# The MLP's steady part of a two-stream hybrid layer: a scheduler's order, and an order written out by hand

## The chip, the cores and the metric

The kernel runs on one core of a Trainium2 chip. The metric is the time of one execution on the device in microseconds (us). The core has a matmul engine (TensorE, PE in the profile, with its weight loads shown apart as PEld), VectorE (DVE), ScalarE (ACT), GpSimd (POOL) and SyncE (SP), which here only starts DMAs. GpSimd starts the DMAs that add to what lies in the buffer. Each engine works through its own queue in order.

## The reference, cut to what matters

One layer is computed for two streams at once, 128 context rows and 512 latent rows, 640 columns in the kernel's transposed layout, with 1024 channels in float32. Three mixers run on an input projection; their outputs are merged, projected by w_out and added to the stream. Then comes the gated MLP, which the change is about (D_FF is 2816, dw_conv is a centred depthwise convolution of width 3):

```python
x = x + gt1 * (merged @ w_o)
h2 = rms_norm(x, n2) * (1 + sc2) + sh2
u_val, u_gate = jnp.split(dw_conv(h2 @ w_up, f_conv), 2, axis=-1)
x = x + gt2 * ((jax.nn.silu(u_gate) * u_val) @ w_dn)
```

## The kernel before

Each float32 matrix product is made of three products of rounded halves: every operand is split into a high part and the rest, and high*high, rest*high and high*rest are accumulated in PSUM. For a weight tile, w_split (L149, L150) casts on ScalarE (wh from raw) and subtracts on VectorE (wl). Weight tiles are loaded by w_load (L140) and st_load (L248 to L252).

The 2816 MLP columns are 22 tiles of 128, f = 0 to 21, in blocks of 4, 4, 4, 4, 3 and 3. The first block (up_tile) is done plainly. From f = 4 on, up_pair makes a value tile and its gate tile together, from seven half-size products of 12 matmuls instead of eight, on sums of weights and sums of activations; the bodies below call them, in order, X, Y, Z, X, Y, Z, Y. Four weight tiles (st, j = 0 to 3) feed a pair; the second and the third hold two sums of weights, of which one is made in flight: SyncE loads a piece (L248), and GpSimd's DMA adds another onto it (L250). VectorE makes the other sums (st_sums: L258 for j = 0, which needs tile 0 and the accumulated half of tile 1, and L260 for j = 2). Three raw buffers and two pairs of wh and wl turn over.

The products are evacuated by ScalarE (L1708, L1718: the copies of X) and VectorE (L1711 to L1733) into two tiles u1 (value) and u2 (gate). finish then convolves each (conv: L506 on ScalarE and four steps, L508, on VectorE), applies the gate (gated: L1651, L1652) and splits the result (split_x: L398, L399).

Between pairs, down multiplies the block before with a 128-row tile of w_down: 24 matmuls for a block of four, 18 for a block of three (gemm_p, L365), and adds the result to the residual stream x1 (two instructions on VectorE, L1759, xa in the rows). A pair is followed by two downs, in the last two blocks by two, three and three; the weights are rawd, whd and wld, two buffers each. At the end, eight downs follow for the last block, each with five transposes (L613), two copies (L1767) and two output DMAs.

What sets the order of the work: all five queues are filled by a scheduler, which goes by dependences and priorities. W looks ahead in a plan of weights (loads up to LOOK_F = 6 ahead where may_load finds a buffer, splits one ahead) and gives loads and splits high priority, as up_pair gives the evacuations. The convolutions and the gate of a pair are a generator, of which some() issues a piece at four places of the next pair.

Of the kernel before, what the change touches and what calls it, by code (L numbers as in the profile page):

```python
# [12 lines left out]
AF = mybir.ActivationFunctionType  # L13
# [45 lines left out]
def hybrid_step(ctx: ExitStack, tc: tile.TileContext, a: dict, o: list):  # L59
# [170 lines left out]

    pidx = {g[0]: i for i, g in enumerate(plan)}
    loaded, split = {}, {}
    LOOK_L, LOOK_S, LOOK_F = 2, 1, 6
    used = [0]


# [3 lines left out]
    def st_load(f, j):  # L240
# [11 lines left out]
            SY.dma_start(out=hi, in_=part(0, 1))  # L252
        return raw

    def st_sums(f, j):

        if j == 0:
            V.tensor_add(st_raw[f, 0][:, 512:], st_raw[f, 0][:, :512], st_raw[f, 1][:, :512])  # L258
        elif j == 2:
            V.tensor_add(st_raw[f, 2][:, 512:], st_raw[f, 0][:, 512:], st_raw[f, 1][:, 512:])  # L260

    def load_of(j):
        key, pieces, kt, n = plan[j]
        return st_load(*key[1:]) if key[0] == "st" else w_load(pieces, kt, n, key[0] == "wd")
# [4 lines left out]
            st_sums(*key[1:])  # L269
        return w_split(loaded[j], kt, n, key[0] == "wd")  # L270

    def may_load(j):

        down = plan[j][0][0] == "wd"
        same = [i for i in range(j) if (plan[i][0][0] == "wd") == down]
        n = 2 if down else RAWB
        if len(same) < n:
            return down
        i = same[-n]
        if i not in split:  # L280
            return False
        key = plan[i][0]
        return key[0] != "st" or key[2] > 1 or pidx["st", key[1], 2] in split

    def W(key):
        i = pidx[key]
        assert i == used[0], (key, i, used[0])
        used[0] += 1
        with tc.high_priority() if i else nullcontext():
            for j in range(i, min(i + LOOK_L + 1, len(plan))):  # L290
                if j not in loaded:
                    loaded[j] = load_of(j)
            for j in range(i, min(i + LOOK_S + 1, len(plan))):
                if j not in split:
                    split[j] = split_of(j)
            if key[0] in ("uv", "ug", "st", "wd"):
                for j in range(i + LOOK_L + 1, min(i + LOOK_F + 1, len(plan))):
                    if j not in loaded:
                        if not may_load(j):
                            break  # L300
                        loaded[j] = load_of(j)
        return split[i]


# [1244 lines left out]
    def ft():  # L1549
        return fslots.pop(0)  # L1550
# [137 lines left out]
            hs[k, i] = rt(2)  # L1688
            split_x(t, *(u[:, :T] for u in hs[k, i]))

    def up_pair(f):

        ps = gtile()
        X, Y, Z = ps[:, :HALF], ps[:, 512:512 + HALF], stile()[:, :HALF]
# [7 lines left out]

        hH2 = h2H, h2L
        u1, u2 = ft(), ft()
        w = W(("st", f, 0))
        prod(X, w, 0, lambda j, k: hH2[j][:, k, L], True, False)
        with tc.high_priority():
            S.copy(u2[:, L], X)  # L1708
        prod(Y, w, 1, lambda j, k: hs[k, 1][j][:, R], True, False)
        with tc.high_priority():  # L1710
            V.tensor_sub(u1[:, R], u2[:, L], Y)  # L1711
        w = W(("st", f, 1))
        prod(Z, w, 0, lambda j, k: hs[k, 0][j][:, L], True, False)
        with tc.high_priority():
            V.tensor_add(u2[:, R], u2[:, L], Z)
        prod(X, w, 1, lambda j, k: hH2[j][:, 4 + k, L], False, True)
        with tc.high_priority():
            S.copy(u1[:, L], X)  # L1718
        some()
        w = W(("st", f, 2))  # L1720
        prod(Y, w, 0, lambda j, k: hs[k, 0][j][:, R], False, False)
        with tc.high_priority():
            V.tensor_sub(u2[:, R], Y, u2[:, R])
        some()
        prod(Z, w, 1, lambda j, k: hH2[j][:, 4 + k, R], False, True)
        with tc.high_priority():
            V.tensor_add(u1[:, R], u1[:, R], Z)
        some()
        some()
        w = W(("st", f, 3))  # L1730
        prod(Y, w, 0, lambda j, k: hs[k, 1][j][:, L], False, True)
        with tc.high_priority():
# [48 lines left out]
    e1x.close()  # L1781
    e2 = ctx.enter_context(tc.tile_pool(name="e2", bufs=1, reuse_waits="tile"))
    slots.extend(e2.tile([P, T + 2], F32R, name=f"r{i}") for i in range(24, 32))
    for b in range(1, NB_F):
        for i in range(FBLK[b]):
            up_pair(fst[b] + i)
            for nt in downs(b, i):
                down(b - 1, nt)
    while later:
        some()  # L1790
    for nt in range(8):
        down(NB_F - 1, nt)


# [32 lines left out]
```

## Time and profile before

| | |
|---|---|
| median of three runs | 1421.82 us (1420.29 to 1423.12) |
| profiled execution | 1424.66 us |
| its span | 1422.9 us |
| TensorE busy | 1330.2 us, 93% |
| VectorE busy | 891.1 us, 63% |
| ScalarE busy | 578.9 us, 41% |
| GpSimd busy | 217.7 us, 15% |
| DMA | 137.97 MB, 97 GB/s in the mean |

The profile is that of one execution; its span is counted from the first to the last thing on the core, and the execution's own time is 1.8 us longer. A matmul's end is modelled, and neighbours overlap, so the spacing of starts tells more than durations. The part that the change is about begins at about 983 us with the first pair and goes to the end of the span.

### The profile page before, as it was taken

To read this page: it belongs to the slowest core of one execution; us is meant where nothing else is said; L and a number is where in the kernel's file an instruction comes from. 1 tells how busy PE (TensorE), PEld (TensorE's weight loads), DVE (VectorE), ACT (ScalarE), POOL (GpSimd) and SP (SyncE) were. 2 spreads that over 40 slices of the span, in tenths; PEclk is the share of its full clock that TensorE was granted. 3 is DMA by queue.
4 is the path that set the end of the run, shared out by engine and by line. 5 is a ranking of instruction groups with operands and counts; after the bars stand their busy time and mean duration, and the time that the engine had idled before them with its cause. 6 is when DMAs were issued, how large, how long until landed. Compare 5 with 4: busy or idle time off the path is not lost.

```text
span 1422.9 us, 27064 instructions
## 1 busy us (share of the span) xinstructions
PE 1330.2 (93%) x10985; PEld 1243.6 (87%) x10985; DVE 891.1 (63%) x1863; ACT 578.9 (41%) x1080; POOL 217.7 (15%) x224
## 2 busy tenths in 40 slices
PE   5999899998989899999999999989899999999898
PEld 4899899998878788999998898988898888988887
DVE  4675876785788553344343344498768677676764
ACT  4543334422675432343333234474334333333333
POOL 1011112203215211012120041100110111101000
PEclk9999999999999999999999999999999999999999
DMA  9523331222011144344344535222544545544323
GB/s 283 151 60 94 82 79 42 56 81 62 20 43 38 39 106 126 91 110 123 85 136 141 149 96 161 70 67 41 114 112 104 104 119 106 109 112 95 94 65 110
DMA packets 228079, 137.97 MB, mean 97 GB/s; under 512 B 22037, under 2 KB 221491, under 8 KB 227955
## 3 DMA queue, kind: packets, MB, share of 16 engines
q1 hardware_dynamic: 208563, 126.48, 32.7%
q0 software_dynamic: 19008, 9.44, 5.4%
q8 instruction: 86, 1.41, 0.4%
q10 hardware_dynamic: 384, 0.33, 0.1%
q14 instruction: 38, 0.31, 0.1%
HBM read 129.67 MB, written 6.55 MB: 96 GB/s over the span
## 4 chain that ended last, share of the span: by engine, by line
PE 50%; DVE 17%; DMA 10%; issue 5%; ACT 3%; POOL 3%; ACTq 0%; SPq 0%; POOLq 0%; DVEq 0%
PE g L365 30%; DMA raw<-in_w_up_dram 9%; PE g L1700 5%; DVE t L508 4%; DVE wl L150 3%; PE g L386 2%; PE s L1700 2%; DVE xa L1759 1%; PE s L613 1%; PE s L413 1%; PE s L1439 1%; DVE wld L150 1%; PE s L1427 1%; ACT wh L149 1%; POOL ssn L335 1%
## 5 line engine op out<-in xcount | busy, mean ns | idle before, releaser
L149 ACT CAST wh<-raw 128x1024 fp32r<-128x1024 f32 (+1 forms) x176 | 164.7, 945 | 358.4 <-PE g L365 179.4
L150 DVE TENSOR_TENSOR wl<-raw,wh 128x1024 fp32r<-128x1024 f32 (+1 forms) x176 | 192.3, 1101 | 153.3 <-ACT wh L149 143.3
L365 PE MATMUL g<-hH,wh 128*128 128x320 f32 x768 | 186.8, 322 | 3.4 <-ACT wh L149 1.9
L365 PE MATMUL g<-hL,wh 128*128 128x320 f32 x768 | 183.9, 317 | 0.0
L365 PE MATMUL g<-hH,wl 128*128 128x320 f32 x768 | 182.3, 316 | 0.0
L365 PE MATMUL g<-r,whd 128*128 128x320 f32 x704 | 139.2, 317 | 10.8 <-DVE t L1733 8.7
L365 PEld LDWEIGHTS g<-hH,wh 128*128 128x128 f32 x768 | 129.1, 191 | 11.5 <-issue 3.9
L365 PEld LDWEIGHTS g<-hL,wh 128*128 128x128 f32 x768 | 130.7, 191 | 2.5 <-issue 1.9
L365 PEld LDWEIGHTS g<-hH,wl 128*128 128x128 f32 x768 | 131.1, 191 | 2.0 <-issue 1.8
L365 PEld LDWEIGHTS g<-r,whd 128*128 128x128 f32 x704 | 111.8, 191 | 16.7 <-DVE t L1733 12.9
L250 POOL DMA_DIRECT2D raw<-in_w_up_dram x36 | 46.4, 1290 | 386.9 <-DMA raw<-in_w_up_dram 294.2
L1700 PE MATMUL g<-r,wh 128*128 128x320 f32 x432 | 101.6, 321 | 3.7 <-ACT t L1708 3.7
L386 PE MATMUL g<-wh,hH 128*128 128x256 f32 x320 | 95.0, 297 | 3.4 <-DVE xb L721 3.4
L386 PE MATMUL g<-wl,hH 128*128 128x256 f32 x320 | 94.5, 295 | 0.0
L386 PE MATMUL g<-wh,hL 128*128 128x256 f32 x320 | 94.5, 295 | 0.0
L1700 PEld LDWEIGHTS g<-r,wh 128*128 128x128 f32 x432 | 70.4, 188 | 12.8 <-ACT t L1708 7.6
L365 PE MATMUL g<-r,wld 128*128 128x320 f32 x352 | 81.0, 311 | 0.0
L508 DVE SCALAR_TENSOR_TENSOR t<-t,fcols,t 128x511 f32<-128x511 f32 (+1 forms) x156 | 78.5, 543 | 3.4 <-ACT t L506 2.9
L365 PE MATMUL g<-oz,wh 128*128 128x320 f32 x384 | 73.8, 314 | 1.3 <-DVE xb L1300 1.2
L386 PEld LDWEIGHTS g<-wh,hH 128*128 128x128 f32 x320 | 63.3, 198 | 5.2 <-DVE xb L721 3.6
L1700 PE MATMUL g<-r,wl 128*128 128x320 f32 x216 | 66.7, 309 | 0.0
L386 PEld LDWEIGHTS g<-wl,hH 128*128 128x128 f32 x320 | 63.7, 199 | 0.0
(592 smaller groups left out, 2902.3 us busy)
## 6 DMA issues: line engine op xcount, KB each, us to landing
raw<-in_w_in_dram SPq DMA_DIRECT2D x64, 512.0 KB
raw<-in_w_up_dram SPq DMA_DIRECT2D x90, 256.0 KB
wada<-in_w_ada_dram SPq DMA_DIRECT2D x32, 512.0 KB
raw<-in_w_up_dram POOLq DMA_DIRECT2D x36, 256.0 KB, 4.7
wat<-in_w_ada_dram SPq DMA_DIRECT2D x16, 512.0 KB
rawd<-in_w_down_dram SPq DMA_DIRECT2D x32, 256.0 KB
raw<-in_w_branch_dram SPq DMA_DIRECT2D x24, 256.0 KB
raw<-in_w_out_dram SPq DMA_DIRECT2D x8, 512.0 KB
```

What stands on the lines that cost most here:

```text
L149: S.copy(wh[:, :m], raw[:, :m])
L150: V.tensor_sub(wl[:, :m], raw[:, :m], wh[:, :m].bitcast(F32))
L250: G.dma_start(out=lo, in_=part(1, 2 - j), accum_op=ALU.add)
L335: G.tensor_tensor(out=out, in0=out, in1=mh.broadcast_to([P, n]), op=ALU.pow)
L365: PE.matmul(out=ps[:, OFF + c0:OFF + c1], lhsT=ww[:, k, :], rhs=xx(k)[:, c0:c1], start=(k == 0 and i == 0), stop=(k == kt - 1 and i == 2))
L386: PE.matmul(out=ps[b][:, o:o + GRP], lhsT=xx[:, 4 * kh + k, cs], rhs=ww[:, k, :], start=(kh == 0 and c % 2 == 0 and k == 0 and i == 0), st ...
L413: PE.matmul(out=pa[32 * g:32 * g + 32, :w], lhsT=csil[:, k, :], rhs=t[g], start=start, stop=stop)
L508: V.scalar_tensor_tensor(out=y[:, o0:o1], in0=src[:, i0:i0 + o1 - o0], scalar=w3(t), in1=y[:, o0:o1], op0=ALU.mult, op1=ALU.add)
L613: PE.transpose(pt[:, i * P:(i + 1) * P], src[:, (c0 + i) * P:(c0 + i + 1) * P], ident)
L1427: PE.transpose(pt[:, i * P:(i + 1) * P], Pt[:, i * P:(i + 1) * P], ident)
L1439: PE.matmul(out=po[64 * e:64 * e + 64, 0:P], lhsT=v[:, h * HD:(h + 1) * HD], rhs=PT[:, i * P:(i + 1) * P], start=(i == 0), stop=(i == len( ...
L1700: PE.matmul(out=out, lhsT=ww[:, 4 * kh + k, :], rhs=xx(hl_, k), start=start and k == 0 and i == 0, stop=stop and k == 3 and i == 2, skip_g ...
```

## The change

In the steady part and the last eight downs, the queues of VectorE, ScalarE and TensorE now follow the program's own order (tc.manual_schedule); SyncE's and GpSimd's are still the scheduler's. The program is rewritten to state that order. W no longer looks ahead in this part; need_load, need_split and st_sums stand by hand beside the product they are to lie with. The gate's convolution (conv_u) of pair f is issued behind the first product of pair f + 1, the gate's silu and multiply behind the fourth, the split behind the fifth; the value's convolution is issued behind the last product of its own pair. Down weights are asked for two downs ahead. After the last pair stands last_gate, then the eight downs, each with the split of the next one's weights ahead of it. The instructions themselves are the same.

```diff
+    st_done = set()
+
     def st_sums(f, j):
 
+        if (f, j) in st_done or ("st", f, 0) not in pidx:
+            return
+        st_done.add((f, j))
         if j == 0:
+            need_load(("st", f, 0), ("st", f, 1))
             V.tensor_add(st_raw[f, 0][:, 512:], st_raw[f, 0][:, :512], st_raw[f, 1][:, :512])
         elif j == 2:
+            need_load(("st", f, 2))
             V.tensor_add(st_raw[f, 2][:, 512:], st_raw[f, 0][:, 512:], st_raw[f, 1][:, 512:])
...
-    def may_load(j):
-
-        down = plan[j][0][0] == "wd"
-        same = [i for i in range(j) if (plan[i][0][0] == "wd") == down]
-        n = 2 if down else RAWB
-        if len(same) < n:
-            return down
-        i = same[-n]
-        if i not in split:
-            return False
-        key = plan[i][0]
-        return key[0] != "st" or key[2] > 1 or pidx["st", key[1], 2] in split
+    def need_load(*keys):
+        for key in keys:
+            j = pidx.get(key)
+            if j is not None and j not in loaded:
+                with tc.high_priority():
+                    loaded[j] = load_of(j)
+
+    def need_split(key):
+        j = pidx.get(key)
+        if j is not None and j not in split:
+            need_load(key)
+            split[j] = split_of(j)
 
     def W(key):
         i = pidx[key]
         assert i == used[0], (key, i, used[0])
         used[0] += 1
+        if key[0] in ("st", "wd"):
+            need_split(key)
+            return split[i]
...
-            if key[0] in ("uv", "ug", "st", "wd"):
-                for j in range(i + LOOK_L + 1, min(i + LOOK_F + 1, len(plan))):
...
+    def conv_u(u, f2):
+        y = ft()
+        conv(y, u, lambda tap, f2=f2: fcols[:, tap, f2:f2 + 1])
+        fslots.append(u)
+        return y
+
+    open_ = {}
+    wds = [g[0] for g in plan if g[0][0] == "wd"]
+
+    def up_pair(f, dn):
...
         w = W(("st", f, 0))
         prod(X, w, 0, lambda j, k: hH2[j][:, k, L], True, False)
-        with tc.high_priority():
-            S.copy(u2[:, L], X)
+        if prev:
+            fp, yv, u2p = prev
+            yg = conv_u(u2p, NF + fp)
+        S.copy(u2[:, L], X)
+        need_split(("st", f, 1))
         prod(Y, w, 1, lambda j, k: hs[k, 1][j][:, R], True, False)
-        with tc.high_priority():
-            V.tensor_sub(u1[:, R], u2[:, L], Y)
+        st_sums(f, 2)
+        need_load(("st", f, 3), ("st", f + 1, 0))
+        V.tensor_sub(u1[:, R], u2[:, L], Y)
         w = W(("st", f, 1))
         prod(Z, w, 0, lambda j, k: hs[k, 0][j][:, L], True, False)
-        with tc.high_priority():
-            V.tensor_add(u2[:, R], u2[:, L], Z)
+        need_split(("st", f, 2))
+        need_load(("st", f + 1, 1))
+        V.tensor_add(u2[:, R], u2[:, L], Z)
         prod(X, w, 1, lambda j, k: hH2[j][:, 4 + k, L], False, True)
-        with tc.high_priority():
-            S.copy(u1[:, L], X)
-        some()
+        if prev:
+            S.activation(out=yg, in_=yg, func=AF.Silu)
+            V.tensor_mul(yv, yv, yg)
+            fslots.append(yg)
+        S.copy(u1[:, L], X)
         w = W(("st", f, 2))
         prod(Y, w, 0, lambda j, k: hs[k, 0][j][:, R], False, False)
-        with tc.high_priority():
-            V.tensor_sub(u2[:, R], Y, u2[:, R])
-        some()
+        need_split(("st", f, 3))
+        need_load(("st", f + 1, 2))
+        if prev:
+            ac[fp] = rt(2)
+            split_x(yv, *(t[:, :T] for t in ac[fp]))
+            fslots.append(yv)
...
+        need_split(dn[0])
+        V.tensor_add(u1[:, R], u1[:, R], Z)
         w = W(("st", f, 3))
         prod(Y, w, 0, lambda j, k: hs[k, 1][j][:, L], False, True)
-        with tc.high_priority():
-            V.tensor_sub(u2[:, L], Y, u2[:, L])
-        later.append(finish(f, u1, u2))
-
-    def finish(f, u1, u2):
-
-        ys = []
-        for u, f2 in ((u2, NF + f), (u1, f)):
-            ys.append(ft())
-            conv(ys[-1], u, lambda tap, f2=f2: fcols[:, tap, f2:f2 + 1])
-            fslots.append(u)
-            yield
-        gated(f, ys[1], ys[0])
-        fslots.extend(ys)
-        yield
-
-    later = []
-
-    def some():
-        if later:
-            if next(later[0], 0) == 0:
-                later.pop(0)
+        open_["prev"] = f, conv_u(u1, f), u2
...
+        for i, key in enumerate(dn):
+            if i == 0:
+                st_sums(f + 1, 0)
+                need_split(("st", f + 1, 0))
+            if i + 1 < len(dn):
+                need_split(dn[i + 1])
+            if i == len(dn) - 1:
+                need_split(("st", f + 1, 1))
+            down(*key[1:])
+            need_load(*wds[wds.index(key) + 2:wds.index(key) + 3])
+
+    def last_gate():
+        fp, yv, u2p = open_.pop("prev")
+        yg = conv_u(u2p, NF + fp)
+        gated(fp, yv, yg)
 
     def down(b, nt):
         ps = gtile()
+        if b == NB_F - 1:
+            for n in (nt, nt + 1):
+                need_split(("wd", b, n))
+            need_load(("wd", b, nt + 2))
...
-    for b in range(1, NB_F):
-        for i in range(FBLK[b]):
-            up_pair(fst[b] + i)
-            for nt in downs(b, i):
-                down(b - 1, nt)
-    while later:
-        some()
-    for nt in range(8):
-        down(NB_F - 1, nt)
+    with tc.manual_schedule(engines={nc.vector.engine, nc.scalar.engine, nc.tensor.engine}):
+        need_load(*wds[:2])
+        for b in range(1, NB_F):
+            for i in range(FBLK[b]):
+                up_pair(fst[b] + i, [("wd", b - 1, nt) for nt in downs(b, i)])
+        last_gate()
+        for nt in range(8):
+            down(NB_F - 1, nt)
```

How the queues differ is shown at three places. First VectorE between two pairs of the steady part. In the names, raw is a weight tile as loaded, wh and wl its two halves, rawd, whd and wld the same of w_down, xa the residual stream, g and s PSUM tiles, t and r work tiles. Before, from the sum for the next pair's first tile on:

```order
L258 TENSOR_TENSOR raw_1539_13050<-raw_1539_13050,raw_1540_13052 128x512
L508 SCALAR_TENSOR_TENSOR t3_9522<-t1_9520,fcols_242,t3_9522 128x511
L1733 TENSOR_TENSOR t2_9521<-g_1530_13007,t2_9521 128x320
L260 TENSOR_TENSOR raw_1543_13091<-raw_1539_13050,raw_1540_13052 128x512
L150 TENSOR_TENSOR wl_1551_13180<-raw_1539_13050,wh_1550_13179 128x1024
L150 TENSOR_TENSOR wl_1555_13212<-raw_1540_13052,wh_1554_13211 128x1024
L1759 SCALAR_TENSOR_TENSOR xa3_485<-g_1546_13146,modc_252,xa3_485 128x512
L150 TENSOR_TENSOR wld_1567_13332<-rawd_1559_13248,whd_1566_13331 128x512
L1759 SCALAR_TENSOR_TENSOR xa3_485<-g_1546_13146,modc_252,xa3_485 128x128
```

After, from the same sum on:

```order
L264 TENSOR_TENSOR raw_1493_12653<-raw_1493_12653,raw_1496_12672 128x512
L150 TENSOR_TENSOR wl_1503_12751<-raw_1493_12653,wh_1502_12750 128x1024
L150 TENSOR_TENSOR wld_1505_12755<-rawd_1489_12616,whd_1504_12754 128x512
L1782 SCALAR_TENSOR_TENSOR xa6_488<-g_1506_12758,modc_252,xa6_488 128x512
L1782 SCALAR_TENSOR_TENSOR xa6_488<-g_1506_12758,modc_252,xa6_488 128x128
L150 TENSOR_TENSOR wl_1509_12788<-raw_1496_12672,wh_1508_12787 128x1024
L1782 SCALAR_TENSOR_TENSOR xa4_486<-g_1510_12791,modc_252,xa4_486 128x512
L1782 SCALAR_TENSOR_TENSOR xa4_486<-g_1510_12791,modc_252,xa4_486 128x128
```

The evacuation L1733 and a convolution step stood behind the sum, and two of the next pair's splits ahead of the first down's xa (from g_1546); the wld after it, wld_1567, is for a down of the next pair. Now the wld that stands third, wld_1505, is for the second of these two downs, whose xa (from g_1510) ends the rows, and the second of the next pair's splits stands between the xa of the two.

Second, ScalarE at the last gate (L506 and L510 are the convolution's first step, L1651 and L1655 the silu, r26 the gated result's high part). Before:

```order
L506 ACTIVATE t6_9525<-t4_9523,fcols_242 128x640
L506 ACTIVATE t0_9519<-t2_9521,fcols_242 128x640
L149 CAST whd_1693_14448<-rawd_1687_14405 128x384
L149 CAST whd_1697_14475<-rawd_1691_14425 128x384
L149 CAST whd_1701_14516<-rawd_1695_14452 128x384
L1651 ACTIVATE t0_9519<-t0_9519 128x640
L398 CAST r26_10793<-t6_9525 128x640
L149 CAST whd_1707_14554<-rawd_1699_14479 128x384
```

After:

```order
L149 CAST whd_1687_14425<-rawd_1677_14301 128x384
L149 CAST whd_1691_14452<-rawd_1690_14450 128x384
L510 ACTIVATE t5_9524<-t3_9522,fcols_242 128x640
L1655 ACTIVATE t5_9524<-t5_9524 128x640
L402 CAST r26_10790<-t4_9523 128x640
L149 CAST whd_1698_14512<-rawd_1694_14477 128x384
L149 CAST whd_1700_14516<-rawd_1696_14500 128x384
```

The first cast for the last block's downs, whd_1701, stood ahead of the silu. Now the first two such casts, whd_1698 and whd_1700, stand behind the silu and behind r26.

Third, TensorE in the last eight downs (s from ident and xa are the transposes). Before:

```order
L365 MATMUL g_1724_14667<-r6_9532,wld_1720_14631 128x320 x2
L365 MATMUL g_1724_14667<-r24_10791,whd_1719_14630 128x320
L613 MATMUL s_1722_14656<-ident_146,xa4_486 128x128 x4
L365 MATMUL g_1724_14667<-r24_10791,whd_1719_14630 128x320
L365 MATMUL g_1724_14667<-r25_10792,whd_1719_14630 128x320
L613 MATMUL s_1723_14662<-ident_146,xa4_486 128x128
L365 MATMUL g_1724_14667<-r25_10792,whd_1719_14630 128x320
L365 MATMUL g_1724_14667<-r24_10791,wld_1720_14631 128x320 x2
L365 MATMUL g_1724_14667<-r26_10793,whd_1719_14630 128x320 x2
```

After:

```order
L369 MATMUL g_1717_14629<-r27_10791,whd_1712_14592 128x320 x2
L369 MATMUL g_1717_14629<-r26_10790,wld_1713_14593 128x320 x2
L617 MATMUL s_1721_14656<-ident_146,xa4_486 128x128 x4
L617 MATMUL s_1722_14662<-ident_146,xa4_486 128x128
L369 MATMUL g_1723_14667<-r6_9532,whd_1718_14630 128x320 x2
L369 MATMUL g_1723_14667<-r7_9533,whd_1718_14630 128x320 x2
L369 MATMUL g_1723_14667<-r6_9532,wld_1719_14631 128x320 x2
```

The transposes of one down lay among the matmuls of the next, four of them behind its seventh matmul. Now they stand right behind the last matmul of their own down.

## Rows read from the trace of the kernel before

**Rows 1.** Windows: stretch, then each engine's busy time, granted clock, DMA share.

```profile
1010.63:1272.66 262.03, 246.31 (x1588) 232.81 (x1586) 193.10 (x327) 101.63 (x146) 30.80 (x24) 1.00 0.49 109
...
1003.36:1006.77 3.41, 3.10 (x11) 3.10 (x12) 3.41 (x6) 2.66 (x3) 0.00 (x0) 0.50 0.53 67
```

**Rows 2.** Timeline of TensorE, a pair's first product: start, duration, what, idle before.

```profile
1161.63 0.39 PE L1700 MATMUL g<-h2H,wh 128*128 128x320 f32 x1 [0.71 <-DVE xa L1759]
1161.86 0.30 PE L1700 MATMUL g<-h2L,wh 128*128 128x320 f32 x1
...
1163.32 0.31 PE L1700 MATMUL g<-h2H,wl 128*128 128x320 f32 x1
```

**Rows 3.** Waits of TensorE, 1010.63 to 1272.66: total, times, longest.

```profile
PE g L1700 <- DVE xa L1759: 9.6, 12, 1.4
```

**Rows 4.** Timeline of SyncE, GpSimd and VectorE over one pair.

```profile
1147.04 0.37 SPq L248 DMA_DIRECT2D raw<-in_w_up_dram  x1
...
1150.71 1.29 POOL L250 DMA_DIRECT2D raw<-in_w_up_dram  x1 [17.44 <-DMA raw<-in_w_up_dram]
...
1152.72 1.28 POOL L250 DMA_DIRECT2D raw<-in_w_up_dram  x1 [0.72 <-DVE t L1727]
1155.34 0.69 DVE L258 TENSOR_TENSOR raw<-raw,raw 128x512 f32<-128x512 f32 x1 [3.36 <-DMA raw<-in_w_up_dram]
...
1161.26 3.73 SPq L140 DMA_DIRECT2D rawd<-in_w_down_dram  x2
1161.41 1.92 DVE L508 SCALAR_TENSOR_TENSOR t<-t,fcols,t 128x511 f32<-128x511 f32 x4
...
1168.79 0.37 SPq L248 DMA_DIRECT2D raw<-in_w_up_dram  x1
```

**Rows 5.** Groups by line and shape, 1010.63 to 1272.66: busy us, mean ns.

```profile
L150 DVE TENSOR_TENSOR wl<-raw,wh 128x1024 fp32r<-128x1024 f32 x36 | 42.9, 1220 | 0.4
...
L149 ACT CAST wh<-raw 128x1024 fp32r<-128x1024 f32 x36 | 36.6, 1050 | 56.3 <-DVE raw L258 39.7 <-PE g L1700 16.5
...
L150 DVE TENSOR_TENSOR wld<-rawd,whd 128x512 fp32r<-128x512 f32 x24 | 16.3, 680 | 0.0
```

**Rows 6.** The accumulating loads' line (L250), 24 of them, 1010 to 1273.

```profile
DMA to landing us min/median/max: 4.5/4.7/4.9
```

**Rows 7.** Timeline of ScalarE: first copies of X, four intervals apart.

```profile
1272.66 0.41 ACT L1708 COPY t<-g 128x320 f32<-128x320 f32 x1
...
1372.15 0.43 ACT L1708 COPY t<-g 128x320 f32<-128x320 f32 x1 [0.90 <-PE g L1700]
```

**Rows 8.** Timeline of VectorE and TensorE in the first pair.

```profile
990.39 0.82 DVE L399 TENSOR_TENSOR r<-gx,r 128x640 fp32r<-128x640 f32 x1
...
1003.67 1.44 PE L365 MATMUL g<-r,whd 128*128 128x320 f32 x4 [2.78 <-DVE t L1733]
```

**Rows 9.** Timeline of TensorE in the stage of w_out.

```profile
860.14 1.12 PE L613 MATMUL s<-ident,t 128*128 128x128 f32 x4 [1.35 <-DMA t<-in_x_sample_dram]
```

**Rows 10.** Timeline of TensorE and VectorE, last Y product and last downs.

```profile
1382.93 0.45 PE L365 MATMUL g<-r,wld 128*128 128x320 f32 x2
...
1407.30 0.75 DVE L1759 SCALAR_TENSOR_TENSOR xa<-g,modc,xa 128x512 f32<-128x512 f32 x1 [1.81 <-PE g L365]
...
1410.59 0.75 DVE L1759 SCALAR_TENSOR_TENSOR xa<-g,modc,xa 128x512 f32<-128x512 f32 x1 [1.81 <-PE g L365]
...
1418.05 0.74 PE L613 MATMUL s<-ident,xa 128*128 128x128 f32 x5 [0.94 <-DVE xa L1759]
```

**Rows 11.** Timeline of ScalarE and VectorE, the last gate and a cast behind.

```profile
1389.71 0.74 ACT L1651 ACTIVATE t<-t 128x640 f32<-128x640 f32 x1
...
1391.78 0.82 DVE L1652 TENSOR_TENSOR t<-t,t 128x640 f32<-128x640 f32 x1 [0.46 <-DVE t L508]
1392.64 0.73 ACT L398 CAST r<-t 128x640 fp32r<-128x640 f32 x1 [2.19 <-DVE t L1652]
...
1394.91 0.51 ACT L149 CAST whd<-rawd 128x384 fp32r<-128x384 f32 x1 [1.55 <-PE g L365]
```

More of the change, by code (lines that the diff above doesn't have):

```diff
@@ L232, in hybrid_step @@
     loaded, split = {}, {}
-    LOOK_L, LOOK_S, LOOK_F = 2, 1, 6
+    LOOK_L, LOOK_S = 2, 1
     used = [0]
@@ L295, in W @@
                     split[j] = split_of(j)
-            if key[0] in ("uv", "ug", "st", "wd"):
-                for j in range(i + LOOK_L + 1, min(i + LOOK_F + 1, len(plan))):
[L298 to L301, printed above, removed]
         return split[i]
@@ L1689, in sums_h2 @@
             split_x(t, *(u[:, :T] for u in hs[k, i]))
-    def up_pair(f):
+    def conv_u(u, f2):
[6 more added lines that the diff above has]
+    def up_pair(f, dn):
         ps = gtile()
@@ L1704, in up_pair @@
         u1, u2 = ft(), ft()
+        prev = open_.pop("prev", None)
         w = W(("st", f, 0))
         prod(X, w, 0, lambda j, k: hH2[j][:, k, L], True, False)
-        with tc.high_priority():
-            S.copy(u2[:, L], X)
+        if prev:
[3 more added lines that the diff above has]
+        need_split(("st", f, 1))
         prod(Y, w, 1, lambda j, k: hs[k, 1][j][:, R], True, False)
-        with tc.high_priority():
-            V.tensor_sub(u1[:, R], u2[:, L], Y)
+        st_sums(f, 2)
@@ L1725, in up_pair @@
+        V.tensor_sub(u2[:, R], Y, u2[:, R])
         prod(Z, w, 1, lambda j, k: hH2[j][:, 4 + k, R], False, True)
-        with tc.high_priority():
-            V.tensor_add(u1[:, R], u1[:, R], Z)
-        some()
-        some()
+        need_split(dn[0])
+        V.tensor_add(u1[:, R], u1[:, R], Z)
         w = W(("st", f, 3))
         prod(Y, w, 0, lambda j, k: hs[k, 1][j][:, L], False, True)
-        with tc.high_priority():
-            V.tensor_sub(u2[:, L], Y, u2[:, L])
-        later.append(finish(f, u1, u2))
@@ L1736, in finish @@
-    def finish(f, u1, u2):
-        ys = []
-        for u, f2 in ((u2, NF + f), (u1, f)):
-            ys.append(ft())
-            conv(ys[-1], u, lambda tap, f2=f2: fcols[:, tap, f2:f2 + 1])
-            fslots.append(u)
-            yield
-        gated(f, ys[1], ys[0])
-        fslots.extend(ys)
-        yield
-    later = []
-    def some():
-        if later:
-            if next(later[0], 0) == 0:
-                later.pop(0)
+        open_["prev"] = f, conv_u(u1, f), u2
+        V.tensor_sub(u2[:, L], Y, u2[:, L])
@@ L1783, in hybrid_step @@
     slots.extend(e2.tile([P, T + 2], F32R, name=f"r{i}") for i in range(24, 32))
-    for b in range(1, NB_F):
-        for i in range(FBLK[b]):
-            up_pair(fst[b] + i)
-            for nt in downs(b, i):
-                down(b - 1, nt)
-    while later:
-        some()
-    for nt in range(8):
-        down(NB_F - 1, nt)
+    with tc.manual_schedule(engines={nc.vector.engine, nc.scalar.engine, nc.tensor.engine}):
[6 more added lines that the diff above has]
+            down(NB_F - 1, nt)
 RPAD = 32
```

## The prediction

> **What bounds the kernel now.** I read the windows view first, to find the stretch that the change touches: the twelve steady pairs with two down products run at full granted clock with TensorE busy 246.31 of 262.03 us [rows 1], that is 21.84 us a pair. Then the matmul spacing: between the second and the twelfth matmul of a product lie ten steps in 1.46 us, 0.146 to 0.147 us each [rows 2]. A pair with two downs has 84 + 48 = 132 matmuls, 19.4 us. So TensorE is not the bound by itself: 2.4 us of a pair are waits. The waits view blames the largest part on xa, VectorE's update of the residual stream, 9.6 us in 12 waits [rows 3]. But VectorE is not full either, so I followed one pair through the timeline of all engines [rows 4]. There the reader is to see a loop that closes on itself:
> - SyncE starts the load of the next pair's second weight tile at 1147.04, when the low split (wl) of this pair's third tile has freed a raw buffer. The accumulating load onto it starts at 1150.71, and VectorE's sum that needs both at 1155.34. Leg C, load to sum: 8.30 us.
> - From the sum to the next pair's first matmul: 1161.63 - 1155.34 = 6.29 us (leg A) [rows 2, 4].
> - From that matmul to the next such load at 1168.79: 7.16 us (leg B).
> The three are 21.75 us, against 21.84 us as the mean: the remaining 0.09 us I add to the pair after too. A pair takes as long as the loop, whatever TensorE could do, so the change is worth what it does to these legs.
>
> **The change in a steady pair.** Nothing is computed more or less; three queues now follow the program's order.
>
> Leg A grows. The second down's wld, which VectorE made a pair ahead, now stands behind the low split of the next pair's first tile, and this behind the sum. From the sum's start: sum 0.69 and 0.10 to ScalarE, cast 1.05 and 0.05 back, low split at a queued spacing of 1.14 (1.22 less 0.08), wld 0.68 and 0.05 to TensorE [rows 4, 5]: 3.76 us. The second down has four matmuls that need no wld; the fifth waits, and 20 remain: 2.94 us, and about 0.1 us to restart. Leg A is 6.8 us, 0.5 us longer. TensorE would have come to the fifth matmul 1.9 us earlier, so this is the stall of the new pair; the waits on xa at the pair's start go, since the first down's xa is now long done when X starts.
>
> Leg B shrinks. Xa of the second down waits for the end of that product (0.26), takes 0.92, four convolution steps 1.92 less overlap, the third tile's sum 0.65, 0.14 to ScalarE, cast 1.06, 0.05, low split 1.22, 0.02: about 6.14 us. Before, a gate multiply and others stood between, and the cast waited for TensorE. This is 1.0 us shorter.
>
> Leg C takes the same loads, at 8.30 us plus something, which I call d. The wd loads, which before started at 1161.26 and so beside the down products, are now asked for when their predecessor is split, by my walk 10.8 us into the pair, and then flow while the accumulating load flows. The trace of before has no such meeting of whole tiles. Bounds: from issue to landing 4.5 us at best and 4.9 at worst around a median of 4.7 [rows 6], so d is at least -0.2; a second tile of the same size wholly in the way costs about as long as one flows, so 0.9 at most. I take 0.35, nearer to the landings seen.
>
> The loop after is 6.81 + 6.14 + 8.30 + 0.09 + 0.35 = 21.69 us, 0.15 less than 21.84. A second floor stands close by: VectorE itself, which must finish Y3's conv and evacuation before the sum, reaches it 14.56 us into the pair, which makes 21.4 us at the least: six products at twelve matmuls 10.56, to the add behind the sixth 0.26, add 0.5, the value's conv on ScalarE 0.9, its four steps on VectorE 1.9, Y3's evacuation 0.4, and then the rest of the loop, 6.8. Twelve intervals: -1.8 us (-5.6 to +4.8).
>
> The same legs, with the down products' own length, give the others, read from one X copy to the next [rows 7]. Two intervals have three downs (24 matmuls more, 3.53): 25.2 each. Two have downs of 18 matmuls, two and three of them (six matmuls less, 0.88, and then 18 more, 2.65): 20.8 and 23.5. Together 94.7, against 1372.15 - 1272.66 = 99.49; but before also did ten matmuls of later downs there, 1.5 us, which I take off: -3.3. The last pair up to its last product: -0.3. The steady part without its first pair: about -5.4 us.
>
> **Its start.** The first pair must now run Y in place. Y's operand is last split on VectorE at 990.39, and the matmuls which before filled the time until then came from a down product [rows 8]. TensorE now idles about 5 us before Y, where before it idled 2.78 us at the pair's end [rows 8]. That gap was followed by 3.41 us at a granted clock of 0.50, 1.2 of 2.4 GHz [rows 1], and I take the same behind the new one; the down's matmuls come after Y3. About 2.2 us more idle stand against waits of the old order that go: laid out by the same durations, the next pair's X comes 0.4 to 0.9 us later: +0.9 (-0.5 to +2.5). Earlier, in the stage of w_out, two w_down loads no longer stand ahead of an x load for which TensorE waited 1.35 us [rows 9]: -1.0 (-2.1 to +0.5).
>
> **Its end** is where I expect the loss. Before, from the end of the last Y product, where a down goes on (1382.93), to the end of the span (1422.9) are 39.97 us [rows 10], 41.4 us with the ten matmuls done early. After:
> - Three downs of the block before, 54 matmuls: 7.94 us.
> - Then the last gate, now behind all three. On VectorE its convolution stands behind the third down's xa, on ScalarE the first casts for the last block's weights stand behind its silu and its cast. So: product to xa 0.26, xa 0.92, four convolution steps 1.84, silu 0.1 + 0.74, multiply 0.05 + 0.82, cast 0.1 + 0.73, whd cast 0.51 [rows 4, 11]: TensorE is idle for about 6.1 us, though 12 of the first down's 18 matmuls need nothing of this gate. Before, this chain ran beside down products.
> - The first down of the last block, 2.65 us at full clock; after such a gap I take the half clock again, 4.2 us.
> - Seven more. Before, each took 3.29 us, as its xa show [rows 10]: 18 matmuls, 2.65, and five transposes at 0.12, with seven matmuls of the next down laid in front of the transposes, so that nothing waits for xa. Now the transposes stand right behind their own down. What this costs is seen at the end of before, where nothing is left to lay between: TensorE stood 0.94 us for xa [rows 10], 1.08 with the product's end and its start. The step becomes 2.65 + 1.08 + 0.6 + 0.1 = 4.43 us; seven are 31.0 instead of 23.0.
> - The last transposes, copy and output as before: 6.1 us.
> Sum 55.3 us, against 41.4: +13.9 us. It is +9 if the clock stays full and the eight waits are half as long, +16 if the short waits bring half clock once more.
> The Trainium skill (TensorE: Matmul & The Clock Gate, Part 2, Step-by-step) says that only weight loads are pulled ahead and that "the MATMULs themselves stay in program order". By that rule no ready matmul slips past a waiting transpose and the step is 4.43; if one did, it would stay near 3.29, 8 us less in all. The 0.94 us of before do not decide it, since nothing was left there to slip past.
>
> **Sum**, against the profiled execution's 1424.66 us (span 1422.9 and 1.8 around it): -5.4 + 0.9 - 1.0 + 13.9 = +8.4 us, 1433 us. The median of the three runs shown is 1421.82, 2.8 below it, and I forecast on that: 1430 us.
>
> **Rivals.**
> 1. The accumulating load is held up by the w_down load beside it (d = 0.9). For it: both now start within 1 us of each other. Against: it shares the time with another accumulating load already, 2 us behind (1152.72), and lands in 4.5 to 4.9 all the same [rows 4, 6]. Price: 0.55 us on 16 pairs, +8.8: 1439 us.
> The Trainium skill (DMA: Bandwidth & Descriptors, Issuing engines are not separate DMA queues) says that DMAs of all issuers run on the same 16 engines and interleave. That is this rival's mechanism; no row of before shows what it costs two whole tiles here.
> 2. On the other side: VectorE reaches the sum and wld without holding the second down, so the new pair loses its 1.9 us stall. Price, 1.9 on 16 pairs: -30, 1400 us. It decides from 0.5 us a pair on, where the 8.4 us are made up. For it: TensorE's own need is 19.4. Against: the accumulating load alone allows 21.3, and VectorE's own queue 21.4.
> 3. The end costs less: the 6.1 us and the clock behind them do not come, because the 12 ready matmuls start. Then the end is +6 and the whole about 1422 us. For it: the operands are there. Against: ScalarE's cast for their weights is queued behind the gate.
>
> **Chances.** Forecast 0.60 (1425 to 1435 on its own), first rival 0.13, second 0.10, third 0.12; 0.05 is left for what I do not see, half of it slower. Within 0.2%, which is what a measurement of this kernel can tell from no change (2.8 us), lie most of the third rival and the lower edge of the forecast: 0.15. Faster 0.11, from the second rival and a little of the third. Slower 0.74. The range holds the forecast, the third rival's upper half and the first rival almost whole: 1420 to 1438 us.
>
> **What would show it.** The new profile should have X copies 21.4 to 22.0 us apart in two-down pairs; TensorE's largest steady wait on DVE wld in the second down instead of on xa; a gap of about 6 us before the last block's first down, ended by whd from ScalarE; last-block xa 4.4 us apart; about 55 us behind the last Y. It would prove me wrong if the X copies are 21.2 or less apart, if the steps at the end stay near 3.3, or if the first pair costs over 3 us.

## The result: slower by 3.7%, and the profile after

The changed kernel takes 1472.41 us (median of four runs, 1470.56 to 1480.98), against 1421.15 us for the kernel before on the same chip: a ratio of 1.037 (95% interval 1.0328 to 1.0413). The direction was forecast; the size was not, and the time lies far above the range. The profiled execution is 1470.56 us, its span 1468.3, 45.4 us more than the span before.

Where the 45.4 us lie is read from ScalarE's first copy of X in each pair; an interval is the time from one pair's copy to the next pair's. The profile before, timeline of ScalarE, the first and the second pair (the fourteenth and the eighteenth are [rows 7]):

```profile
985.02 0.43 ACT L1708 COPY t<-g 128x320 f32<-128x320 f32 x1 [1.01 <-PE g L1700]
1010.63 0.43 ACT L1708 COPY t<-g 128x320 f32<-128x320 f32 x1 [1.42 <-PE g L1700]
```

The profile after, the same four pairs:

```profile
981.59 0.42 ACT L1725 COPY t<-g 128x320 f32<-128x320 f32 x1 [0.98 <-PE g L1714]
1011.45 0.42 ACT L1725 COPY t<-g 128x320 f32<-128x320 f32 x1 [4.70 <-PE g L1714]
...
1298.48 0.42 ACT L1725 COPY t<-g 128x320 f32<-128x320 f32 x1 [4.69 <-PE g L1714]
...
1401.22 0.42 ACT L1725 COPY t<-g 128x320 f32<-128x320 f32 x1 [6.03 <-PE g L1714]
```

| stretch | before, us | after, us | more | forecast |
|---|---|---|---|---|
| up to the first copy of X | 985.02 | 981.59 | -3.4 | -1.0 |
| first interval | 25.61 | 29.86 | +4.2 | +0.9 |
| twelve two-down intervals | 262.03 | 287.03 | +25.0 | -1.8 |
| the next four | 99.49 | 102.74 | +3.2 | -4.8 |
| last copy of X to the end | 50.75 | 67.08 | +16.3 | +15.1 |

(The forecast's credit of 1.5 us for ten matmuls done early stands here in the last row, not in the row above it.) The stage ahead of the steady part proves nothing: in the profiles of the experiments below, whose edits nearly all lie behind it, the first copy comes anywhere between 979.5 and 990.3 us.

So the end is as forecast, and the steady part is not: 23.92 us a pair in the mean instead of 21.69, and the intervals come in two sizes, 23.0 and 24.6 us. Waits of TensorE over the twelve intervals after (total, times, longest), where before xa stood first [rows 3]:

```profile
PE g L369 <- ACT whd L149: 13.2, 12, 1.2
PE g L1714 <- ACT t L1741: 6.2, 12, 0.5
PE g L1714 <- ACT t L1725: 6.2, 12, 0.5
PE g L369 <- DVE wld L150: 5.9, 12, 0.5
```

One pair, TensorE's timeline after: X, the two waits on ScalarE's copies of X, the two downs, and the next X.

```profile
1129.27 0.31 PE L1714 MATMUL g<-h2H,wh 128*128 128x320 f32 x1
...
1131.70 0.56 PE L1714 MATMUL g<-r,wh 128*128 128x320 f32 x2 [0.52 <-ACT t L1725]
...
1137.75 0.56 PE L1714 MATMUL g<-r,wh 128*128 128x320 f32 x2 [0.52 <-ACT t L1741]
...
1143.12 0.74 PE L369 MATMUL g<-r,whd 128*128 128x320 f32 x4
...
1147.89 0.85 PE L369 MATMUL g<-r,whd 128*128 128x320 f32 x4 [1.11 <-ACT whd L149]
1149.24 0.56 PE L369 MATMUL g<-r,wld 128*128 128x320 f32 x2 [0.49 <-DVE wld L150]
...
1153.81 0.31 PE L1714 MATMUL g<-h2H,wh 128*128 128x320 f32 x1
```

And VectorE in the same pair: the add behind the sixth product, the value's convolution, Y3's evacuation, the sum.

```profile
1141.57 0.49 DVE L1753 TENSOR_TENSOR t<-t,s 128x320 f32<-128x320 f32 x1 [0.66 <-PE s L1714]
1143.01 2.19 DVE L512 SCALAR_TENSOR_TENSOR t<-t,fcols,t 128x511 f32<-128x511 f32 x4 [0.96 <-ACT t L510]
1145.12 0.48 DVE L1757 TENSOR_TENSOR t<-g,t 128x320 f32<-128x320 f32 x1
1145.52 0.68 DVE L264 TENSOR_TENSOR raw<-raw,raw 128x512 f32<-128x512 f32 x1
```

The sum starts 1145.52 - 1129.27 = 16.25 us into the pair, straight behind VectorE's own work: no load is waited for any more. Behind the second down's waits the granted clock falls to half, 1.2 of 2.4 GHz (windows view after, that stretch of the pair: length, busy times, clock third from the end; its edges take in a little full clock):

```profile
1149.24:1152.72 3.48, 3.48 (x15) 3.48 (x15) 1.99 (x3) 0.28 (x1) 0.00 (x0) 0.57 0.25 75
```

Summed over half-microsecond windows, the twelve intervals hold 23.9 us at half clock, seven stretches of 3.4 us; before, the same intervals held none [rows 1]. An interval with such a stretch is 1.55 us longer (24.56 against 23.01).

### The profile page after: what moved, and what is told of

Its sections match the earlier page's. It is cut to its first block, busy times and chain, and to the rows that moved or that the text cites. A ratio compares the mean times of both kernels' runs of the same rounds, so it can differ in the third digit from the quotient of the medians.

```text
span 1468.3 us, 27024 instructions
## 1 busy us (share of the span) xinstructions
PE 1340.4 (91%) x10985; PEld 1253.7 (85%) x10985; DVE 900.4 (61%) x1863; ACT 574.6 (39%) x1080; POOL 218.1 (15%) x224
## 4 chain that ended last, share of the span: by engine, by line
PE 61%; DVE 14%; ACT 6%; issue 4%; POOL 3%; DMA 1%; ACTq 0%; SPq 0%; DVEq 0%; POOLq 0%
PE g L369 34%; PE g L1714 9%; PE s L1714 4%; DVE t L512 3%; PE g L390 2%; ACT wh L149 2%; PE s L617 1%; DVE wl L150 1%; PE s L417 1%; PE s L1443 1%; ACT t L510 1%; DVE wld L150 1%; PE s L1431 1%; DVE raw L264 1%; POOL ssn L339 1%
## 5 line engine op out<-in xcount | busy, mean ns | idle before, releaser
L369 PE MATMUL g<-r,whd 128*128 128x320 f32 x704 | 145.4, 332 | 26.3 <-ACT whd L149 26.3
L369 PEld LDWEIGHTS g<-r,whd 128*128 128x128 f32 x704 | 120.1, 205 | 31.1 <-ACT whd L149 31.0
L250 POOL DMA_DIRECT2D raw<-in_w_up_dram x36 | 46.4, 1290 | 420.8 <-DMA raw<-in_w_up_dram 183.2
L369 PE MATMUL g<-r,wld 128*128 128x320 f32 x352 | 88.1, 334 | 8.3 <-DVE wld L150 8.3
L512 DVE SCALAR_TENSOR_TENSOR t<-t,fcols,t 128x511 f32<-128x511 f32 (+1 forms) x156 | 82.2, 548 | 19.8 <-ACT t L510 17.3
L1782 DVE SCALAR_TENSOR_TENSOR xa<-g,modc,xa 128x512 f32<-128x512 f32 x96 | 48.3, 545 | 53.7 <-PE g L369 53.7
L369 PEld LDWEIGHTS g<-r,wld 128*128 128x128 f32 x352 | 64.1, 206 | 12.7 <-DVE wld L150 12.7
```

Source lines behind the costliest of these rows:

```text
L250: G.dma_start(out=lo, in_=part(1, 2 - j), accum_op=ALU.add)
L369: PE.matmul(out=ps[:, OFF + c0:OFF + c1], lhsT=ww[:, k, :], rhs=xx(k)[:, c0:c1], start=(k == 0 and i == 0), stop=(k == kt - 1 and i == 2))
L512: V.scalar_tensor_tensor(out=y[:, o0:o1], in0=src[:, i0:i0 + o1 - o0], scalar=w3(t), in1=y[:, o0:o1], op0=ALU.mult, op1=ALU.add)
```

## Experiments

The theory after the result: (a) two waits on X's copies delay everything in the pair, the sum included; (b) the second down waits for its split, queued behind the sum; (c) half clock follows on that wait. The rivals: the loads bind, or an in-order TensorE is slow whatever the others do. All times are medians, all ratios against the kernel before on the same chip, whose median was 1423.5 to 1426.0 us there. "After" is the changed kernel, 1472.41 us. It was timed beside a kernel before of 1421.15 us, 2 to 5 us less, so the differences from it given below are that much too small; the ratios are not touched by this.

**Y in a PSUM tile of its own.**

```diff
-        X, Y, Z = ps[:, :HALF], ps[:, 512:512 + HALF], stile()[:, :HALF]
+        X, Y, Z = ps[:, :HALF], mtile()[:, :HALF], stile()[:, :HALF]
```

> The changed kernel, with the products called Y in a PSUM tile of their own (a free 512-column tile) instead of the second half of X's. Theory: TensorE stood 0.52 us twice a pair (waits on the two copies of X) because Y is written to the tile that ScalarE still reads; with the slower start behind each wait the products took 13.9 us from X to the first down, where I had forecast 12.35. Then both waits go, X to first down becomes about 12.4 us, VectorE's sum comes 1.4 us earlier in the pair, and a two-down pair is 1.3 us shorter in each, 18 pairs: about -24 us against the changed kernel, near 1448 us. The wait in the second down and the half clock behind it stay. Rival (the accumulating loads set the pair): the waits go, the sum then waits for DMA, and the time moves by under 6 us.

Measured: 1465.71 us, 1.0285 (1.025 to 1.0321): 7 us less, not 24. Both waits are gone, as theory had it; but the pair is 23.5 us. TensorE's waits over the twelve intervals, and one pair's sum:

```profile
PE g L369 <- ACT whd L149: 22.0, 12, 2.4
PE g L369 <- DVE wld L150: 5.6, 12, 0.5
```

```profile
1145.58 0.69 DVE L264 TENSOR_TENSOR raw<-raw,raw 128x512 f32<-128x512 f32 x1 [0.52 <-DMA raw<-in_w_up_dram]
```

The products' gain was lost in the wait of the second down, which grew from 1.10 to 1.83 us in the mean, and half clock followed in 11 of 12 intervals; the one without it is 22.04 us, 1.0 less than at full clock in after. The rival has a part in it: the sum now waits for its load in all twelve pairs, 0.65 us in the mean.

**The second down's split ahead of the sum.**

```diff
             if i == 0:
+                need_split(dn[1])
                 st_sums(f + 1, 0)
```

> The changed kernel, with the split of the second down's weights (whd and wld) placed ahead of the sum for the next pair's first tile on ScalarE and VectorE, instead of behind that tile's split. Theory: the second down's waits (1.1 us for whd, 0.5 for wld) go, and with them the stretches of half clock, 3.4 us each, that follow in 7 of 12 pairs and cost 1.5 us each. TensorE then sets the pair: 13.9 + 7.06 = 21.0 us instead of 23.9 in the mean; 16 pairs: about -45 us, near 1427 us. Rival 1 (loads set the pair, or VectorE's sum comes too late): the wait moves to the next pair's X, waiting for wl, and the pair keeps at least 23.0 us. Rival 2 (the half clock comes from the two short waits on X's copies): it stays, and the pair is about 22 us.

Measured: 1429.43 us, 1.0033 (1.0008 to 1.0058): 43 us less for one line. The timeline of ScalarE's copies of X:

```profile
1133.56 0.43 ACT L1725 COPY t<-g 128x320 f32<-128x320 f32 x1 [2.68 <-PE g L1714]
1154.63 0.43 ACT L1725 COPY t<-g 128x320 f32<-128x320 f32 x1 [2.68 <-PE g L1714]
1175.69 0.43 ACT L1725 COPY t<-g 128x320 f32<-128x320 f32 x1 [2.67 <-PE g L1714]
```

All twelve intervals are 21.06 to 21.08 us, the forecast 21.0, at full clock throughout. TensorE sets the pair, with the two waits on X's copies in it (0.52 each, 18 times). So (b) is shown, the half clock went with the wait as (c) has it, and the short waits on the copies alone bring none.

**The end reordered.** The last gate's convolution ahead of the last pair's downs, the rest of the gate ahead of the second of them, one whd cast ahead of the third, and the transposes one down later:

```diff
+            if last and i == 1:
+                gated(fp, yv, yg)
+            if last and i == len(dn) - 1:
+                need_split(("wd", NB_F - 1, 0))
...
         for nt in range(8):
             down(NB_F - 1, nt)
+            if nt:
+                out_rows(nt - 1)
+        out_rows(7)
```

> The changed kernel, with the end reordered: the last gate's convolution stands ahead of the last pair's downs and the rest of the gate ahead of the second of them, the first cast for the last block's weights ahead of the third, and in the last eight downs each one's transposes stand behind the next down's matmuls. Theory: TensorE's 6.05 us before the last block and its half clock go (about 7.7 us), and the step of the eight downs falls from 4.30 to about 3.3 us (7 us): about -14 us, near 1458 us. Rival (the steps are bound by the split of the next weights or by the output, not by the transposes' place): only the first part goes, -8 us, and the steps stay over 4 us.

Measured: 1463.24 us, 1.026 (1.0238 to 1.0282). In the profile the step is 1444.38 - 1441.19 = 3.19 us and the end 43.0 us from the last Y product, where after has 55.2. The 12 us are there; the median fell by 9. This profile's twelve intervals still hold seven with half clock, and all of the next four do, where in after it is two.

```profile
1441.19 1.01 DVE L1790 SCALAR_TENSOR_TENSOR xa<-g,modc,xa 128x512 f32<-128x512 f32 x2 [1.00 <-PE g L369]
...
1444.38 1.01 DVE L1790 SCALAR_TENSOR_TENSOR xa<-g,modc,xa 128x512 f32<-128x512 f32 x2 [1.00 <-PE g L369]
```

**The convolution's steps in turn** (long, short, long, short; the line that sets the order):

```diff
+        for o0, o1, i0, t in ((1, TS, 0, 0), (TS + 1, T, TS, 0), (0, TS - 1, 1, 2), (TS, T - 1, TS + 1, 2)):
```

> The changed kernel, with the four convolution steps on VectorE in the steady part in the order long, short, long, short, as the scheduler had placed them before, instead of long, long, short, short. Theory: a step that follows on the one that wrote the same columns waits for its end; four steps take 1.92 us instead of 2.18. Two sets of four lie on the way to the sum or to the freed buffer: 0.26 us a pair behind the sum in the one loop that binds, 0.5 at most, so -5 to -9 us, near 1465 us. Rival (VectorE does not set the pair): no difference, under 2 us.

Measured: 1461.57 us, 1.0248 (1.0212 to 1.0284), 11 us less. The intervals are 22.75 us, 0.26 less than the short ones of after, as forecast; the rest was not foreseen: half clock in one interval of twelve instead of seven. The second down waited 0.83 to 0.90 us for whd in the eleven at full clock and 1.67 us in the one with half clock (0.92 in the mean, where after has 1.10).

**Filler matmuls in the second down's wait.**

```diff
+            if i == 1:
+                pm, wq, b0 = mtile(), split[pidx[dn[0]]][0], key[1]
+                for q in range(8):
+                    PE.matmul(out=pm[:, :HALF], lhsT=wq[:, q % FBLK[b0], :], rhs=ac[fst[b0] + q % FBLK[b0]][0][:, :HALF],
+                              start=True, stop=True, skip_group_check=True)
```

> The changed kernel with eight more matmuls per pair, on operands that are there, into a PSUM tile that nothing reads, laid between the first down and the second, where TensorE waits 1.1 us for whd. It does more and can take no wait away. Theory (the half clock follows on that wait, and costs 1.5 us where it comes): the wait is filled, the half clock goes from the steady pairs, and every two-down pair takes 23.0 to 23.3 us instead of 23.0 and 24.6 in turns: -8 us, near 1464 us, although TensorE does more. Rival (the half clock comes from the pair's load as a whole or from the two short waits on X's copies): the intervals stay at 23.0 and 24.6 or get longer, 1472 us or more.

Measured: 1464.95 us, 1.0282 (1.0251 to 1.0312). The twelve intervals take 276.4 us instead of 287.03, with 96 matmuls more. The windows view of a stretch of that length, which starts 7 us ahead of the second pair's copy, has the clock at 1.00:

```profile
1013.10:1289.40 276.30, 257.94 (x1681) 246.13 (x1680) 198.08 (x324) 99.27 (x145) 30.80 (x24) 1.00 0.47 104
```

All but one interval (23.2) are 23.0 us. Work that nothing needs made the kernel faster: (c) by itself.

**Both steady edits** (Y apart and the early split), with no further edit:

> Two of the edits: Y in a PSUM tile of its own and the second down's split ahead of the sum. Theory: alone, the own tile gave 6 us only, since the second down's wait took up what the products gave back and half clock followed in 11 of 12 pairs instead of 7; with that wait gone it gives its full 1.2 to 1.5 us a pair: 19.5 to 19.9 us, 1405 to 1410 us against 1429 with the early split alone. Rival (the loads are next): no pair under 20.5 us, and 1418 us or more.

Measured: 1410.76 us, 0.9909 (0.9876 to 0.9943). The intervals are 19.9 us in the mean, 1.2 us less than with the early split alone. Here the own tile pays in full.

**TensorE's order alone.**

```diff
-    with tc.manual_schedule(engines={nc.vector.engine, nc.scalar.engine, nc.tensor.engine}):
+    with tc.manual_schedule(engines={nc.tensor.engine}):
```

> One part of the change alone: TensorE follows the program's order, VectorE and ScalarE stay with the scheduler. The scheduler puts the sum ahead of the convolution and of the last evacuations and the split of the second down's weights well ahead of that down. Theory (what costs is VectorE's and ScalarE's written order behind the sum, and TensorE's order only the two waits on X's copies and the end): pairs of about 21.0 us as with the early split alone, no half clock in them, a shorter gap before the last block: 1418 to 1430 us. Rival (TensorE's in-order queue is the cost, whatever the others do): pairs of 23 us or more, over 1455 us.

Measured: 1488.79 us, 1.0446 (1.0396 to 1.0496): slower than the whole change. My theory fell here, and the time and the pairs (25.2 us, half clock in nine of twelve) are what the rival gave. But the rival's cause, an in-order TensorE whatever the others do, is ruled out by the runs with the early split: TensorE's order is the same there, at 21.06 and 19.9 us a pair. The scheduler put the sum ahead of the sixth product's add (L1753) and of Y3's evacuation (L1757). VectorE's timeline:

```profile
1152.92 0.49 DVE L1750 TENSOR_TENSOR t<-g,t 128x320 f32<-128x320 f32 x1 [1.77 <-PE g L1714]
1156.80 0.69 DVE L264 TENSOR_TENSOR raw<-raw,raw 128x512 f32<-128x512 f32 x1 [3.38 <-DMA raw<-in_w_up_dram]
1157.41 0.48 DVE L1753 TENSOR_TENSOR t<-t,s 128x320 f32<-128x320 f32 x1
...
1161.73 0.48 DVE L1757 TENSOR_TENSOR t<-g,t 128x320 f32<-128x320 f32 x1
```

The sum stands 3.38 us at the head of the queue, and what TensorE needs stands behind it: it waits for L1757 30.2 us in twelve pairs, at the first matmul of the second down. In before the sum also stood ahead of Y3's evacuation (L1733), and TensorE, whose order the scheduler made too, waited 3.2 us for that. The Trainium skill (PSUM — Partial Sum Buffer, Engine vs sequencer instructions) calls VectorE's queue strictly first in, first out; the rows above agree.

**VectorE's and ScalarE's order alone** (the same line with the other two engines).

> The other part of the change alone: VectorE and ScalarE follow the program's order, TensorE stays with the scheduler, which puts products of the second weight tile between X and Y and lays later matmuls into waits. Theory: the waits on X's copies and most of the end's loss go, but the second down's split stays behind the sum in two queues, and TensorE can only move about it what is ready: pairs of 21.5 to 23.6 us, an end about 10 us shorter than the changed kernel's 55: 1440 to 1460 us. Rival (the cost lies in TensorE's order): near 1420 us.

Measured: 1463.45 us, 1.0253 (1.0204 to 1.0301). The waits on X's copies are gone, since the scheduler lays products of the second tile between X and Y again, and the last copy of X to the end is 58.0 us, 9 less than in after, as forecast. But the pair is 23.92 us all the same: the second down waits 1.72 us for whd in the mean, with half clock in all twelve.

```profile
PE g L369 <- ACT whd L149: 20.6, 12, 1.9
```

The time lies just above the range that I gave. Neither half of the change alone is better than before.

**The own tile in the kernel before.**

> The kernel before, unchanged but for Y in a PSUM tile of its own. Theory: the scheduler hid ScalarE's copies of X behind products of the second tile, so at most the short waits (2.5 us in twelve pairs) can go, and the pair is set by the loads and VectorE: no difference, 1420 to 1425 us. Rival (the shared tile cost the old order too): 5 us or more less.

Measured: 1429.15 us, 1.0027 (0.9992 to 1.0062): no difference that can be told, and no gain. In its profile (1438.32 us, the longest of ten runs) the waits on X's copies are gone from the twelve intervals, but TensorE waits 24.6 us for xa instead of 9.6 [rows 3], and half clock holds for 24 us, where the profile of before has none. So a tile of its own gains nothing in the scheduler's order, where the pair waits for xa; what the shared tile alone costs there stays open.

**All four edits.**

> The four edits together: Y in a PSUM tile of its own, the second down's split ahead of the sum, the end reordered, the convolution steps in turn. Theory: with the second down's wait gone TensorE sets the pair, and with the waits on X's copies gone too its own 132 matmuls do: 19.4 to 19.8 us a pair, 1.3 less than with the early split alone (21.06), no half clock in the steady part; the end 43 us instead of 55. Against the kernel with the early split alone (1429 us): 16 x 1.3 and 12 us less, 1395 to 1400 us, which is below the kernel before. Rival (the loads come next: in the run with Y apart the sum waited for its accumulating load 15.4 us into the pair): pairs of 20.5 us or more, over 1408 us.

Measured: 1392.95 us (1390.62 to 1399.47), 0.9789 (0.9756 to 0.9823): 2.1% less than the kernel before. Windows view, twelve intervals:

```profile
1012.40:1250.10 237.70, 234.19 (x1586) 231.97 (x1585) 191.35 (x325) 99.47 (x144) 30.80 (x24) 1.00 0.54 120
```

TensorE is busy 234 of 238 us. Against the two steady edits it is 18 us less, of which 14 lie behind the last copy of X (51.3 us to the end instead of 65.3 in the profiles). The pair is 19.81 instead of 19.89 us, so the order of the steps adds nothing once TensorE sets the pair. The order written out by hand is worth something with the other three faults mended.

**And Y later in the first pair.**

> The kernel with all four edits, and in the first pair alone Y behind X's second product and Z, as Y's operand is split last. Theory: the first pair's wait for that split (4.3 and 0.6 us) is filled with 24 matmuls, 3.5 us, and the half clock behind it goes in part: 3 to 5 us less than with four edits (1393), near 1389 us. Rival (the wait moves to Z, whose operands are split just before): under 1.5 us.

Measured: 1394.60 us, 0.9784 (0.9732 to 0.9836): no gain. The wait moved, as with the rival, though to X's second product and not to Z: TensorE now waits 1.46 and 1.54 us for the second tile's two halves and 2.05 us later on, 5.05 us in all, where the run with four edits has 4.34 and 0.59.

## Why the prediction was wrong

- **The end** was right, and with it the direction, by its own mechanism and not by luck: 55.2 us from the last Y product (1413.11 to 1468.3) against 55.3, the gap 6.05 against 6.1, the steps 4.30 against 4.43. The third rival, ready matmuls that start, did not come: they stood behind whd on ScalarE. No matmul of the next down started ahead of a waiting transpose either. Timelines of TensorE and VectorE after:

```profile
1413.11 0.75 PE L369 MATMUL g<-r,whd 128*128 128x320 f32 x4
...
1427.31 1.43 PE L369 MATMUL g<-r,whd 128*128 128x320 f32 x4 [6.05 <-ACT whd L149]
...
1436.76 1.01 DVE L1782 SCALAR_TENSOR_TENSOR xa<-g,modc,xa 128x512 f32<-128x512 f32 x2 [1.00 <-PE g L369]
...
1441.08 1.01 DVE L1782 SCALAR_TENSOR_TENSOR xa<-g,modc,xa 128x512 f32<-128x512 f32 x2 [1.00 <-PE g L369]
```

- **Leg A** was right in its length: in an interval at full clock 23.01 - 16.25 = 6.8 us from the sum to the next X. That the second down would wait for its split behind the sum was said, and the early split showed it. But I named wld as the wait; the cast to whd stands behind the sum and the first tile's cast too, and TensorE stood longer for it, 13.2 us against 5.9 for wld.
- **The failed step** is the second floor, "six products at twelve matmuls 10.56", and what it carries. I laid the products end to end and put what lies between them at nothing. Y is written to the other half of the tile that ScalarE copies X from, and in written order nothing lies between; each wait is 0.52 us, and 0.7 with the wider spacing of the matmuls around it. VectorE's add behind the sixth product came at 12.30 us instead of 10.82, its four steps took 2.18 instead of 1.9 in their new order, and the sum started at 16.25, not 14.56. So this path by way of VectorE bound the loop, not the load: 23.0 us, 1.3 more than forecast. Of the 26.8 us that the twelve intervals missed by, this is 15.8. The runs with Y apart and with the steps in turn show both parts. In before the same wait existed, but products of the second tile filled most of it; before's waits over the same twelve intervals as [rows 3] had it (total, times, longest):

```profile
PE g L1700 <- ACT t L1708: 2.5, 8, 0.3
```

- **Left out** was half clock in the steady part: I took it for the two long gaps only. It followed on waits of 1.1 us and adds 0.9 us a pair in the mean (7 x 1.55 / 12), 10.9 of the 26.8 us. The filler run shows it apart from all else.
- **d**, what an accumulating load loses to the load beside it, was about as forecast and did not decide. All accumulating loads together took 4.7 us to land in the median, as before [rows 6], but at most 6.2 instead of 4.9; the one that the sum needs, the first of each pair's two, took 5.07 us in the mean instead of 4.72. It landed 0.94 us ahead of the sum in the mean, so the first rival did not decide either. The load is close behind, though: in the run with Y apart it did come last.

```profile
DMA to landing us min/median/max: 4.3/4.7/6.2
```

- **The first pair** cost 4.2 instead of 0.9 us, over the 3 us that I gave as a sign of being wrong: TensorE stood 3.56 and 0.59 us for Y's operand, with half clock behind, much as forecast, but the two copies and the second down's waits (1.08 and 0.49 us) came on top.
- **The four last intervals** carry the same loop: two are 1.2 and 1.3 us longer than forecast, and the two with half clock 2.7 and 2.9.
- In the stage of w_out TensorE's wait for the x load fell from 1.35 [rows 9] to 0.28 us, as forecast; what that is worth at the end does not show, since the stage's own length varies by more.

What stays open: why half clock follows on some of the waits of 1.1 us in after and not on others.

## What to carry to other kernels

When an order is written out, look at what the scheduler's odd places did: a few matmuls between a product and the next write to the same tile, a weight split made one round ahead. Price every wait that the new order lists, however short: two of 0.5 us moved the whole loop. And before putting a piece beside a product, ask what stands behind it in its queue if its operand is late.

## What the runs showed of the hardware

- Half clock came after short waits too. By the second down's wait for whd, in twelve intervals each of after, Y apart, the steps in turn, and VectorE's and ScalarE's order alone: at 0.83 to 0.90 us none of 11 intervals had a stretch of 3.4 us at half clock, at 1.08 to 1.18 us 7 of 12, at 1.59 to 2.40 us 24 of 25. In the first three of these runs a wait of 0.33 to 0.50 us for wld came behind it. With no wait for whd (filler, early split) none of 24 had it, although two waits of 0.52 us a pair on X's copies stayed.
- Four convolution steps on VectorE took 2.18 us in the order long, long, short, short, where a step stands right behind the one whose columns it reads and writes again, and 1.92 us in turns.
